# A decoder trunk on one core: three engines issue in the order of the text, and weights are split three units ahead

## The chip, the core and the metric

The kernel runs on one core of a Trainium2 chip. The metric is device time in microseconds (us) of one execution. The engines of the core are TensorE (PE: matrix products, into PSUM), VectorE (DVE), ScalarE (ACT), GpSimd (POOL) and SyncE (SP); each takes its instructions from a queue of its own, and DMA transfers are issued from the queues of SP, ACT and POOL. Here the weights' loads are issued from SP's queue.

## The reference

The input is 256 tokens of 2048 numbers in float32. There are two residual layers, each a mixer followed by a feed-forward part, and a last norm:

```
layer 0:  h = rms_norm(x);  z = h @ w_in
          y_a = rwkv7(z[:, :3360])      # 16 heads x 64: token shift, data-dependent decay,
                                        # S = S*w + (S a) b + v k per token, read with r, norm, gate
          y_b = diff_attention(z[...])  # 8 heads, two softmax maps each, rotary positions, 128-wide values
          x = x + concat(y_a, y_b) @ w_out
          h = rms_norm(x);  x = x + (silu(h @ w_gate) * (h @ w_up)) @ w_down    # hidden 5632
layer 1:  z = gelu(rms_norm(x) @ od_in);  u, v = split(z);  v = layer_norm(v)
          x = x + (u * (tril(w_s) v + b)) @ od_out      # w_s: 16 groups of 128 x 128, per chunk of 128 tokens
          h = rms_norm(x);  x = x + (silu(h @ w_gate) * (h @ w_up)) @ w_down
return rms_norm(x)
```

All weights are read once, 401 MB of them. They are float32, and the products are made to about that precision from pairs of a rounded half and a remainder.

## The kernel before, in words

**Tiles and units.** Activations lie transposed, features on the 128 partitions and the 256 tokens along the free axis. An activation tile `act` is 128x512: columns 0 to 255 hold the value rounded to the format fp32r (the hi half), columns 256 to 511 the remainder (the lo half). A projection (`proj_a`, L288) makes 256 output features and goes over its inputs in units of 256 input rows. For a unit, `weights` (L241) gives two parts hi and lo of the weights: ScalarE rounds the loaded tile `st` (L255, `hi`), and VectorE subtracts (L256, `lo`). A unit then has four products of `hi` with all 512 columns of `act` (L302) and four of `lo` with the first 256 (L306), into the PSUM tile `acc`. Every second unit, counted back from the last, does the lo products first, so that eight hi products follow one another. With `wide=False` the products are three times four of 256 columns (L314 to L316). `proj_b` (L327) turns the operands around for results with tokens on the partitions; its units are half as many rows and twice as many columns (L335 to L337).

**Buffers.** There are three `st` buffers of two units each (a load of 512 KB), five `hi`, five `lo`, two `acc` and four small PSUM tiles `sm`. `AHEAD` (L27) says how many split units `weights` keeps in hand beyond the one that it returns: with 1, the split of the next unit stands in the text before the products of this one.

**Stages.** Layer 0 begins with a projection that follows the loading of `x`, the sums of its norm, and the three evacuations that mix each token with the one before (`shifted`). Four quarters of the recurrent part (`quarter`) and two groups of attention (`rope`, `attention`) then run as generators beside the projections that deliver the next ones: after each unit `tick` (L272) advances the first lane by 1.3 steps and the second by 1.1, and `pause` yields steps in which nothing is done. In a quarter, GpSimd stores 8 small pieces of a product to DRAM, loads them back spread out as `DB` and writes ones on its diagonal (L629); VectorE's recursion over 15 rows (L696, L697) begins with that tile, thirteen paused steps and nine others later in the text. The feed-forward part (`ffn`, L424) has 22 pairs of a gate and an up projection of eight units; after the up projection of a pair come `comb_a` for the gate (ScalarE copies half of `acc`, L323; VectorE adds, L324, and multiplies by the norm, L325), Silu (L431), `comb_a` for the up projection, a product (L434) and the two casts and subtractions of the hidden tile (`split`, L285 and L286). Then `out_proj` (L412) has eight projections of 22 units, each followed by two adds to the residual (L414, L416) and, through `Norm.chunk`, by the casts and the square that prepare the next norm. `Norm.end` (L377) makes the reciprocal root from the sums. Layer 1 begins with the loads of two rows, biases and `w_s` on ScalarE's queue (L958, L963, L970); `mixers`, a generator, transposes `w_s` on TensorE (L973).

**What sets the order.** The functions record instructions in the order of the text. A scheduler then orders each engine's queue: it keeps dependencies and buffers, takes the order of the text as priority, and moves an instruction ahead of others that it expects not to be ready, by its own estimate of durations. The semaphores are set afterwards. On the chip every engine goes through its queue in that order.

Of the kernel before, what the change touches and what calls it, by code (L numbers as in the profile page):

```python
# [23 lines left out]
CDEC = math.exp(-0.5)  # L24
RATE_Q = 1.3
RATE_A = 1.1
AHEAD = 1  # L27
XLOAD = (2,2,2,2,2,2,2,2)
XFIRST = 2
Y1 = 2  # L30
# [100 lines left out]
def trunk_kernel(  # L131
# [15 lines left out]
    nc = tc.nc  # L147
    V, S, T, G = nc.vector, nc.scalar, nc.tensor, nc.gpsimd

    cpool = ctx.enter_context(tc.tile_pool(name="cpool", bufs=1))  # L150
    wpool = ctx.enter_context(tc.tile_pool(name="wpool", bufs=4))
    pool = ctx.enter_context(tc.tile_pool(name="pool", bufs=1))
# [88 lines left out]
    def weights(w, row, col):  # L241
        while len(ready) <= AHEAD and (halves or plan):
            if not halves:
                src, r, nr, c, ncol = plan.popleft()
                n = nr * ncol // 128
                st = wpool.tile([128, 1024], F32, tag="st", name=nm("st"), bufs=3)[:, :n]
                nc.sync.dma_start(st, wts[at[0] : at[0] + 128 * n].rearrange("(p f) -> p f", p=128))
                at[0] += 128 * n
                nh = 2 if nr == 512 or ncol > 256 else 1
                for h in range(nh):  # L250
                    halves.append((st[:, h * n // nh : (h + 1) * n // nh], n // nh, ncol, (src, r + h * nr // nh, c)))
            half, n, ncol, key = halves.popleft()
            hi = wpool.tile([128, 512], F32R, tag="hi", name=nm("hi"), bufs=5)
            lo = wpool.tile([128, 512], F32R, tag="lo", name=nm("lo"), bufs=5)
            S.copy(hi[:, :n], half)  # L255
            V.tensor_sub(lo[:, :n], half, hi[:, :n])  # L256
            ready.append(([(hi[:, k : k + ncol], lo[:, k : k + ncol]) for k in range(0, n, ncol)], key))
        parts, key = ready.popleft()
        assert key == (w, row, col), (key, w, row, col)
        return parts  # L260
# [872 lines left out]
```

## Time and profile before

| | |
|---|---|
| median of 3 runs | 2350.4 us (2349.5 to 2353.93) |
| profiled execution | 2349.51 us, span 2347.7 us, granted TensorE clock 0.992 of full |
| TensorE busy | 2291.3 us, 98% |
| VectorE, ScalarE, GpSimd busy | 1531.8, 1197.4, 66.4 us |
| DMA | 414.08 MB, 176 GB/s |

TensorE is the engine to look at: busy time of the others costs nothing while it works. Where it pauses, the timeline and the list of waits say what ended the pause. A line of the waits names the instruction that waited, the one that it waited for, the total, how often and the longest. TensorE's products are pipelined, so the distance between two starts says more than the length of one.

### The profile page before, as it was taken

The page shows a single profiled execution, that of the slowest core. Times are in us where ns is not written, and L with a number is a line of the kernel's source. Part 1 is how long each engine was busy: PE and PEld are TensorE (multiplying, and loading weights), DVE is VectorE, ACT ScalarE, POOL GpSimd, SP SyncE. Part 2 cuts the span into 40 slices and gives each one's busy share as a digit, 9 for nine tenths or more (in the row PEclk, how much of TensorE's full clock was granted, in tenths as well). Part 3 has the DMA queues.
Part 4 walks back from the last instruction along what each step waited for, and adds up shares of the span by engine and source line. Part 5 has one row for each costly group of instructions (what it writes and reads, how often), then busy time and mean ns, then how long its engine had stood idle before and what let it go on. Part 6 is the DMA issues. An engine that isn't in the chain of part 4 may idle for free.

```text
span 2347.7 us, 39701 instructions
## 1 busy us (share of the span) xinstructions
PE 2291.3 (98%) x14878; PEld 2008.8 (86%) x14878; DVE 1531.8 (65%) x2845; ACT 1197.4 (51%) x2230; POOL 66.4 (3%) x96
## 2 busy tenths in 40 slices
PE   8898989899999999999999999999999999999997
PEld 8887887688888888888888888888888888888887
DVE  7667776688766666665555558776666666665554
ACT  6445544556555555554444455555555555544443
POOL 0000000002000000000000000010000000000000
PEclk9999999999999999999999999999999999999999
DMA  6544344435566665656666765566666666656664
GB/s 217 144 135 123 117 124 146 115 113 185 183 189 189 188 189 188 189 189 188 189 189 188 244 194 176 177 188 181 192 190 189 187 188 191 190 189 189 189 189 135
DMA packets 121105, 414.08 MB, mean 176 GB/s; under 512 B 14160, under 2 KB 18384, under 8 KB 120400
## 3 DMA queue, kind: packets, MB, share of 16 engines
q1 hardware_dynamic: 113664, 401.00, 55.1%
q0 software_dynamic: 2112, 4.46, 0.9%
q10 hardware_dynamic: 5136, 6.09, 0.8%
q8 instruction: 116, 1.90, 0.3%
q14 instruction: 77, 0.63, 0.1%
HBM read 409.14 MB, written 2.36 MB: 175 GB/s over the span
## 4 chain that ended last, share of the span: by engine, by line
PE 77%; DVE 2%; issue 1%; DMA 1%; ACT 0%; POOL 0%; DVEq 0%; POOLq 0%; ACTq 0%
PE acc L302 46%; PE acc L306 24%; PE acc L314 1%; PE acc L315 1%; PE acc L316 1%; PE acc L337 1%; PE acc L336 1%; PE acc L335 1%; DVE lo L256 1%; ACT hi L255 0%; DMA AT<-in_w_s 0%; PE sm L1026 0%; DMA st<-in_wts 0%; PE sm L742 0%; DVE xres L1043 0%
## 5 line engine op out<-in xcount | busy, mean ns | idle before, releaser
L256 DVE TENSOR_TENSOR lo<-st,hi 128x512 fp32r<-128x512 f32 (+1 forms) x1520 | 1048.6, 694 | 618.6 <-ACT hi L255 613.8
L255 ACT CAST hi<-st 128x512 fp32r<-128x512 f32 (+1 forms) x1520 | 927.3, 618 | 947.3 <-PE acc L302 606.6
L302 PE MATMUL acc<-H,hi 128*128 128x512 f32 x3560 | 901.2, 393 | 0.0
L302 PEld LDWEIGHTS acc<-H,hi 128*128 128x128 f32 x3560 | 639.2, 189 | 113.3 <-issue 0.3
L306 PEld LDWEIGHTS acc<-H,lo 128*128 128x128 f32 x3560 | 486.2, 190 | 44.4 <-DVE lo L256 9.3
L306 PE MATMUL acc<-H,lo 128*128 128x256 f32 x3560 | 501.5, 283 | 9.1 <-DVE lo L256 9.1
L316 PE MATMUL acc<-H,lo 128*128 128x256 f32 x488 | 141.7, 290 | 14.6 <-DVE lo L256 14.5
L314 PE MATMUL acc<-H,hi 128*128 128x256 f32 x488 | 144.1, 295 | 8.4 <-ACT hi L255 8.4
L315 PE MATMUL acc<-H,hi 128*128 128x256 f32 x488 | 140.9, 289 | 0.0
L336 PE MATMUL acc<-lo,H 128*128 128x512 f32 (+1 forms) x320 | 126.1, 394 | 6.5 <-DVE lo L256 6.5
L335 PE MATMUL acc<-hi,H 128*128 128x512 f32 (+1 forms) x320 | 129.6, 405 | 0.0
L337 PE MATMUL acc<-hi,H 128*128 128x512 f32 (+1 forms) x320 | 125.7, 393 | 0.0
L316 PEld LDWEIGHTS acc<-H,lo 128*128 128x128 f32 x488 | 96.1, 197 | 15.9 <-DVE lo L256 15.5
L302 PE MATMUL acc<-AT,hi 128*128 128x512 f32 x400 | 105.7, 396 | 0.0
L314 PEld LDWEIGHTS acc<-H,hi 128*128 128x128 f32 x488 | 96.0, 197 | 11.2 <-ACT hi L255 8.4
L302 PE MATMUL acc<-RB,hi 128*128 128x512 f32 x392 | 101.7, 392 | 0.0
L324 DVE TENSOR_TENSOR TR<-acc,TA 128x512 f32<-128x512 f32 x96 | 66.0, 688 | 54.3 <-ACT TA L323 54.3
L315 PEld LDWEIGHTS acc<-H,hi 128*128 128x128 f32 x488 | 96.0, 197 | 0.6 <-issue 0.3
L323 ACT COPY TA<-acc 128x512 f32<-128x512 f32 x96 | 56.1, 584 | 60.6 <-PE acc L302 60.6
L302 PEld LDWEIGHTS acc<-AT,hi 128*128 128x128 f32 x400 | 72.0, 189 | 13.7 <-issue 0.3
L302 PEld LDWEIGHTS acc<-RB,hi 128*128 128x128 f32 x392 | 70.5, 189 | 12.8
L336 PEld LDWEIGHTS acc<-lo,H 128*128 128x128 f32 x320 | 61.1, 191 | 17.4 <-DVE lo L256 6.9
(330 smaller groups left out, 2057.4 us busy)
## 6 DMA issues: line engine op xcount, KB each, us to landing
st<-in_wts SPq DMA_DIRECT2D x740, 512.0 KB, 3.6
st<-in_wts SPq DMA_DIRECT2D x20, 256.0 KB, 2.7
DB<-scr POOLq DMA_DIRECT2D x4, 1024.0 KB, 13.7
st<-in_wts SPq DMA_DIRECT2D x8, 416.0 KB, 3.3
xres<-in_x SPq DMA_DIRECT2D x8, 256.0 KB, 5.8
RB<-in_rows ACTq DMA_DIRECT2D x8, 256.0 KB, 6.1
AT<-in_b_s ACTq DMA_DIRECT2D x4, 256.0 KB, 6.4
AT<-in_w_s ACTq DMA_DIRECT2D x4, 256.0 KB, 8.2
```

Of the source, the lines that this page charges most:

```text
L255: S.copy(hi[:, :n], half)
L256: V.tensor_sub(lo[:, :n], half, hi[:, :n])
L302: T.matmul(acc[:, m, :], hi, acts[2 * u + k], start=first and k == 0, stop=last and k == 1)
L306: T.matmul(acc[:, m, 0:256], lo, acts[2 * u + k][:, 0:256], start=False, stop=False)
L314: T.matmul(acc[:, m, 0:256], hi, act[:, 0:256], start=first and k == 0, stop=False)
L315: T.matmul(acc[:, m, 0:256], hi, act[:, 256:512], start=False, stop=False)
L316: T.matmul(acc[:, m, 0:256], lo, act[:, 0:256], start=False, stop=last and k == 1)
L323: S.copy(t3, acc[:, :nmt, 256:512])
L324: V.tensor_add(dst, acc[:, :nmt, 0:256], t3)
L335: T.matmul(acc[:, t, :ncol], xh, hi, start=k == 0, stop=False)
L336: T.matmul(acc[:, t, :ncol], xh, lo, start=False, stop=False)
L337: T.matmul(acc[:, t, :ncol], xl, hi, start=False, stop=k == last)
```

## The change

```diff
-AHEAD = 1
+AHEAD = 3
 XLOAD = (2,2,2,2,2,2,2,2)
...
     V, S, T, G = nc.vector, nc.scalar, nc.tensor, nc.gpsimd
 
+    ctx.enter_context(tc.manual_schedule(engines={mybir.EngineType.PE, mybir.EngineType.DVE, mybir.EngineType.Activation}))
     cpool = ctx.enter_context(tc.tile_pool(name="cpool", bufs=1))
```

TensorE, VectorE and ScalarE now issue their instructions as the text records them; the scheduler still orders the queues of SyncE and GpSimd. DMAs that ScalarE issues stand where the text has them too. `weights` splits three units ahead of the one it returns; the five hi and lo buffers are unchanged. The added line moves all later lines down by one, so that L255 becomes L256.

The first place is ScalarE's queue at the end of a pair of the first feed-forward layer. `TA<-acc` is the copy of half a projection's result, `TR<-TR` Silu, `H` a hidden tile, `hi` a rounded unit of weights. Before:

```order
L255 CAST hi_11763<-st_11761 128x512
L255 CAST hi_11794<-st_11761 128x512
L255 CAST hi_11808<-st_11806 128x512
L255 CAST hi_11820<-st_11806 128x512
L323 COPY TA_11782<-acc_11670 128x512
L255 CAST hi_11834<-st_11832 128x512
L255 CAST hi_11846<-st_11832 128x512
L255 CAST hi_11860<-st_11858 128x512
L255 CAST hi_11872<-st_11858 128x512
L285 CAST H_11787<-TR_11781 128x256
L285 CAST H_11790<-TR_11781 128x256
L255 CAST hi_11886<-st_11884 128x512
```

Now, for the same pair:

```order
L256 CAST hi_11749<-st_11747 128x512
L256 CAST hi_11761<-st_11747 128x512
L256 CAST hi_11775<-st_11773 128x512
L324 COPY TA_11788<-acc_11577 128x512
L432 ACTIVATE TR_11787<-TR_11787 128x512
L324 COPY TA_11794<-acc_11682 128x512
L286 CAST H_11799<-TR_11793 128x256
L286 CAST H_11802<-TR_11793 128x256
L256 CAST hi_11806<-st_11773 128x512
L256 CAST hi_11820<-st_11818 128x512
```

The copies, Silu and the casts of a pair stood between splits and stand now in one block, behind the splits of three units of the next pair and ahead of the fourth (`hi_11806`). The gate's copy and its Silu, which stood among the up projection's splits, have moved behind all of these.

The second place is VectorE's queue at the end of another pair of that layer. `TR<-acc,TA` is the add, `TR<-TR,rb` the product with the norm, `AT` and `H` are hidden tiles. Before:

```order
L324 TENSOR_TENSOR TR_11325<-acc_11214,TA_11326 128x512
L256 TENSOR_TENSOR lo_11379<-st_11376,hi_11378 128x512
L325 TENSOR_TENSOR TR_11325<-TR_11325,rb_7099 128x512
L256 TENSOR_TENSOR lo_11391<-st_11376,hi_11390 128x512
L434 TENSOR_TENSOR TR_11325<-TR_11325,TR_11319 128x512
L256 TENSOR_TENSOR lo_11405<-st_11402,hi_11404 128x512
L256 TENSOR_TENSOR lo_11417<-st_11402,hi_11416 128x512
L286 TENSOR_TENSOR AT_11331<-TR_11325,AT_11331 128x256
L286 TENSOR_TENSOR H_11334<-TR_11325,H_11334 128x256
L256 TENSOR_TENSOR lo_11431<-st_11428,hi_11430 128x512
```

Now:

```order
L257 TENSOR_TENSOR lo_11320<-st_11317,hi_11319 128x512
L325 TENSOR_TENSOR TR_11331<-acc_11121,TA_11332 128x512
L326 TENSOR_TENSOR TR_11331<-TR_11331,rb_7111 128x512
L325 TENSOR_TENSOR TR_11337<-acc_11226,TA_11338 128x512
L326 TENSOR_TENSOR TR_11337<-TR_11337,rb_7111 128x512
L435 TENSOR_TENSOR TR_11337<-TR_11337,TR_11331 128x512
L287 TENSOR_TENSOR AT_11343<-TR_11337,AT_11343 128x256
L287 TENSOR_TENSOR H_11346<-TR_11337,H_11346 128x256
L257 TENSOR_TENSOR lo_11351<-st_11317,hi_11350 128x512
```

The adds and products of both projections and the two subtractions have drawn together between the third unit's split and the fourth's.

The third place is ScalarE's queue where layer 1 begins. `AT<-in_b_s` are bias loads, `AT<-in_w_s` the four loads of `w_s`. Before:

```order
L963 DMA AT_14520<-in_b_s 128x512
L255 CAST hi_14473<-st_14471 128x512
L970 DMA AT_14535<-in_w_s 128x4x128
L255 CAST hi_14525<-st_14471 128x512
L970 DMA AT_14556<-in_w_s 128x4x128
L255 CAST hi_14546<-st_14544 128x512
L970 DMA AT_14575<-in_w_s 128x4x128
L255 CAST hi_14565<-st_14544 128x512
L970 DMA AT_14596<-in_w_s 128x4x128
L255 CAST hi_14586<-st_14584 128x512
L365 ACTIVATE H_14490<-xres,vc 128x256
```

Now:

```order
L350 ACTIVATE TA_14508<-xres 128x512
L959 DMA RB_14510<-in_rows 128x512
L959 DMA RB_14512<-in_rows 128x512
L959 DMA RB_14514<-in_rows 128x512
L959 DMA RB_14516<-in_rows 128x512
L959 DMA RB_14518<-in_rows 128x512
L959 DMA RB_14520<-in_rows 128x512
L959 DMA RB_14522<-in_rows 128x512
L959 DMA RB_14524<-in_rows 128x512
L964 DMA AT_14526<-in_b_s 128x512
```

Before, the twelve row and bias loads and the four of `w_s` stood between splits, ahead of the last casts and square of the old norm (L365). Now they follow that square (L350), all twelve in a row; behind three more bias loads come the split of a unit and the first load of `w_s`, and each later load of `w_s` behind one more split.

## Rows read from the trace of the kernel before

**Rows 1.** The page: busy us (share of the span) and instructions, by engine.
```profile
PE 2291.3 (98%) x14878; PEld 2008.8 (86%) x14878; DVE 1531.8 (65%) x2845; ACT 1197.4 (51%) x2230; POOL 66.4 (3%) x96
```

**Rows 2.** Busy time by stretch: engines, granted clock, DMA share, GB/s.
```profile
60.00:120.00 60.00, 52.09 (x430) 48.55 (x429) 38.45 (x98) 28.75 (x60) 5.26 (x10) 0.94 0.53 149
...
600.00:1000.00 400.00, 400.00 (x2292) 351.97 (x2292) 258.99 (x412) 210.01 (x376) 0.00 (x0) 1.00 0.62 190
```

**Rows 3.** Waits of TensorE: us in total, times, longest.
```profile
PE acc L316 <- DVE lo L256: 14.5, 3, 7.8
...
PE acc L306 <- DVE lo L256: 9.1, 1, 9.1
...
PE acc L336 <- DVE lo L256: 6.5, 1, 6.5
```

**Rows 4.** Timeline: start us, us, what [idle before], at the first quarter's L696.
```profile
107.17 0.17 DVE L696 TENSOR_TENSOR sub<-DB,inv 128x16 f32<-128x16 f32 x1 [11.73 <-POOL DB L629]
...
111.11 0.58 PE L316 MATMUL acc<-H,lo 128*128 128x256 f32 x1 [7.75 <-DVE lo L256]
...
111.49 0.41 PE L314 MATMUL acc<-H,hi 128*128 128x256 f32 x1
...
111.70 0.41 PE L315 MATMUL acc<-H,hi 128*128 128x256 f32 x1
...
115.26 0.28 PE L314 MATMUL acc<-H,hi 128*128 128x256 f32 x1
...
115.38 0.28 PE L315 MATMUL acc<-H,hi 128*128 128x256 f32 x1
```

**Rows 5.** Timeline: a boundary of the first feed-forward layer.
```profile
775.11 2.00 PE L302 MATMUL acc<-H,hi 128*128 128x512 f32 x8
...
776.24 0.59 ACT L323 COPY TA<-acc 128x512 f32<-128x512 f32 x1 [1.26 <-PE acc L302]
...
777.90 2.00 PE L302 MATMUL acc<-H,hi 128*128 128x512 f32 x8
```

**Rows 6.** Groups by form: busy us, mean ns of one, idle before.
```profile
L256 DVE TENSOR_TENSOR lo<-st,hi 128x512 fp32r<-128x512 f32 x1496 | 1035.8, 697 | 613.2 <-ACT hi L255 608.5 <-PE acc L315 1.5
...
L324 DVE TENSOR_TENSOR TR<-acc,TA 128x512 f32<-128x512 f32 x96 | 66.0, 688 | 54.3 <-ACT TA L323 54.3
...
L434 DVE TENSOR_TENSOR TR<-TR,TR 128x512 f32<-128x512 f32 x44 | 30.2, 685 | 0.0
...
L255 ACT CAST hi<-st 128x512 fp32r<-128x512 f32 x1496 | 915.8, 620 | 936.5 <-PE acc L302 606.6 <-PE acc L315 66.5 <-issue 62.8
...
L323 ACT COPY TA<-acc 128x512 f32<-128x512 f32 x96 | 56.1, 584 | 60.6 <-PE acc L302 60.6
...
L431 ACT ACTIVATE TR<-TR 128x512 f32<-128x512 f32 x44 | 27.6, 627 | 0.0
...
L285 ACT CAST RB<-TR 128x256 fp32r<-128x256 f32 x28 | 10.1, 401 | 0.0
```

**Rows 7.** Groups by form: a product of the norm's root.
```profile
L189 DVE TENSOR_TENSOR TR<-rb 128x256 f32<-128x256 f32 x12 | 5.1, 422 | 0.2
```

**Rows 8.** Timeline: ScalarE issues a row load.
```profile
1294.37 0.34 ACTq L958 DMA_DIRECT2D RB<-in_rows  x1
```

**Rows 9.** DMA issues: count, KB each, median us to landing.
```profile
DB<-scr POOLq DMA_DIRECT2D x4, 1024.0 KB, 13.7
...
RB<-in_rows ACTq DMA_DIRECT2D x8, 256.0 KB, 6.1
...
AT<-in_w_s ACTq DMA_DIRECT2D x4, 256.0 KB, 8.2
...
sk<-in_lam ACTq DMA_DIRECT2D x1, 128.0 KB, 4.5
```

**Rows 10.** Timeline of TensorE at the first transposes of w_s.
```profile
1316.00 0.66 PE L973 MATMUL sm<-c,AT 128*128 128x128 f32 x4 [1.57 <-DMA AT<-in_w_s]
...
1316.72 0.39 PE L336 MATMUL acc<-lo,H 128*128 128x512 f32 x1
```

## The prediction

> **What bounds the kernel now.** I read the page's busy shares first. TensorE is busy 2291.3 of the span's 2347.7 us [rows 1], so the whole idle time that any order of issue could give back is 56 us. The busy time by stretch says where it lies: in the feed-forward stretch from 600 to 1000 us TensorE is busy all 400, while between 60 and 120 us it is idle for 8 and its granted clock is 0.94 of the 2.4 GHz level [rows 2]. The waits of TensorE name what ends that idle time: a lo half from VectorE, 14.5, 9.1 and 6.5 us, with single waits of up to 9.1 [rows 3]. The timeline of one of them gives the cause. VectorE stood 11.73 us at L696, the recursion for the inverse, until GpSimd had written the ones into the gathered diagonal; every split queued behind it came late, TensorE waited 7.75 us, and the products that followed started 0.21 us apart (111.49, 111.70) where later ones start 0.12 apart (115.26, 115.38): 3.8 us at half rate, so the wait cost another 1.8 us [rows 4]. There is one such place in each of the four quarters. The rest of the kernel is a TensorE that never waits, because the evacuations of one projection stand between the splits of the next on ScalarE and VectorE.
>
> The sum is made against the profiled execution's own 2349.5 us, within 1 us of the median 2350.4.
>
> **What the change gives.** In the text, 22 steps of a quarter lie between the gather's loads and L696 (nine yields and the pause of 13). At 1.3 steps for each unit that is 17 units of 1.4 us, 24 us, and the quarter's own products lie between them too. The gather takes 13.7 us to land [rows 9] and the eight small loads before it several more, about 21 together, so VectorE should find it done. That takes away the three lines of [rows 3], 30 us, and four times 1.8 us of slow clock: **-37 us**. It can't be more than the idle total allows, and if a quarter's wait stays it is 9 less.
>
> **What it costs: the feed-forward boundary.** In the rows of the order, the gate's copy, its Silu, the up projection's copy and the two casts of the hidden tile now stand in one block on ScalarE, and the next split after them is that of the fourth unit of the next projection (U3). On VectorE the same holds of the add, two products, two subtractions. Let T0 be the end of the up projection. A unit is (777.90-775.11)/2 = 1.395 us and ScalarE sees TensorE's end 0.20 us late (two units are eight products of 512 columns and eight of 256, so four of 512 take a third of 2.79, 0.93; they start at 775.11 and end at 776.04, and the copy starts at 776.24) [rows 5]. The durations are those of [rows 6].
> The hi cast of U2 needs the buffer of the up projection's sixth unit, free at T0-2.79; it runs from -2.59 to -1.97. The gate's copy ends at -1.39, lo of U2 at -1.27, the add at -0.58, the product with the norm at 0.11, Silu at 0.74. Only then does ScalarE take the up projection's copy, to 1.32. The add ends at 2.01, the two products at 3.38, the two casts at 4.18, hi of U3 at 4.80, lo of U3 at 5.50. TensorE has U0 to U2, 3 x 1.395 = 4.18 us, and U3 is one of the units that begin with lo. It waits 1.3 us, with about 0.03 at each change of engine 1.5. There are 44 boundaries: 44 x 1.5 = **+66 us**. Low end: if the gate's part is out of the way when T0 comes, 0.5 less each, 41; high end 2.0 each, 88. After the wait ScalarE and VectorE need 1.3 of every 1.395 us at most and are three units ahead again before the next boundary.
>
> **Other projections.** At a boundary of an output projection the same chain is two adds, two scaled casts, a square and the split: 0.20 + 2 x 0.69 + 2 x 0.40 + 0.63 + 0.62 + 0.70 = 4.3 us (adds taken as long as L324, casts as L285, the square as L431 [rows 6]) against 4.18, hence 0.1 to 0.4 at about 30 boundaries. In the second pass over w_out a projection has only three units, 4.18 us, and VectorE 3 x 0.7 + 2 x 0.69 + 2 x 0.42 = 4.3 us of work: perhaps 0.8 each, eight times. Together +14 (6 to 24). The eight boundaries of the gated unit have copy, add, product, Gelu, add, product, casts and split, 6.3 us, less 4.18 and the mixing products: +10 (5 to 15).
>
> **Norms.** A norm's reciprocal root is thirteen VectorE operations of at most 0.42 us [rows 7], a chain of about 5 us that stood between splits before and is now one block. In the feed-forward layers U3 comes 1.9 us late, twice. Before the gated unit TensorE itself waits for the chain, 5.5 us, and loses 1.8 to the clock. Together +13 (8 to 18).
>
> **The start.** TensorE begins when four units are split rather than two, 3 us. The eight squares and fifteen adds of the first norm (8 x 2 x 0.42 = 6.7 us of VectorE) stand before the fourth unit of a projection with half-wide units, whose three units cover 2.1: 5 us. Then the norm's chain, on which TensorE waits 5.7; behind it ScalarE issues the load of the lambdas, 4.5 us to land [rows 9], VectorE waits for it, and three shifted evacuations (each some 2 us, two engines in turn) stand before U3: about 21 us from the end of the projection, of which three units cover 4.2. With two slow-clock stretches: 20. Together **+28** (12 to 40).
>
> **The loads of the gated unit.** ScalarE issues eight row loads and four bias loads, 0.34 us each [rows 8], then splits U3, then issues the first load of w_s, which takes 8.2 us [rows 9]; TensorE's transposes of it stand behind the projection's first unit. T0 + 3 for the last adds and casts, 4 for issuing, 0.6, 8.2 gives 16 us, and 20 if the later row loads must wait for the first to land (6.1). TensorE waits 14 to 18 us there, and the fourth of these loads is issued only when TensorE has gone on, some 5 us more. Before, it waited 1.57 [rows 10]. **+25** (12 to 30).
>
> **The recurrent and attention part.** Here the trace of before shows no such wait, since small products stood wherever their operands were ready. I walked one quarter. The four tanh, a split and two squares on ScalarE (about 0.5 each) stand before a product one unit later: 2 us. The small reciprocal root and a copy: 1. Five 512-wide VectorE operations, as long as the 0.685 of L434 [rows 6], four 256-wide ones and three splits stand between the transposes and the products that need them, 9 us against four units at most: 4 to 5. The inverse's thirty small operations, some 8 us with splits between them, in five steps: 2. Since the rate is 1.3, about 15 of 64 steps follow another directly, half of these hand a result from TensorE to another engine and back, 0.6 each: 4. That is 14 a quarter, 57, and eight attention heads and four rotary pairs delay VectorE by 2 to 4 us each, of which perhaps 1 shows: **+70**. Bounds: 20 if the pauses in the text cover most of it, 110 if attention delays every chain. I take 70, the value of the quarter walked.
>
> **Sum.** -37 + 66 + 14 + 10 + 13 + 28 + 25 + 70 = 189; 2349.5 + 189 = **2540 us**.
>
> **The clock as a rule.** After a wait of 1.57 us the products of 512 columns still took 0.39 and the clock stayed granted in full [rows 10], after 7.75 it did not [rows 4]; so I price the short feed-forward waits without a loss of clock. The Trainium skill (TensorE: Matmul & The Clock Gate, Part 1) says that the array's default state is throttled and that activity releases it, which speaks against any change that adds idle time; by it, repeated waits might lower the clock each time. This case's trace bears it out for the long wait alone.
>
> **Rivals.**
> - *The short waits lower the clock.* Each feed-forward boundary would lose another 1.8 us, 44 x 1.8 = 79: 2620 us. Against it stands [rows 10]. Chance 0.08.
> - *The pauses fit the text.* The recurrent part costs 20 rather than 70 and the start and loads half of theirs: 2540 - 50 - 27 = 2463, say 2460. For it: the steps and pauses are counted in units, which only an issue by the text keeps. Chance 0.14.
> - *Three units ahead hide the chain* (the other side). If the fourth unit's lo half were there before T0 + 4.18, the feed-forward part, two thirds of the kernel, would cost nothing, and with the 37 us given back and small costs at the start the time would be 2330. The point is 4.18 us; my chain is at 5.5 and would have to lose a quarter. Chance 0.06.
> - *The costs are right in kind but small, and cancel.* 2350. Chance 0.03.
> - That the change does not do what it says is excluded by the rows of the order.
>
> The forecast has 0.69, with 2460 to 2610 for itself. The bounds added up go from 2420 to 2645; all low or all high at once is unlikely, so the range is 2440 to 2620. A measurement can tell about 0.2%, 5 us: faster 0.06, same 0.03, slower 0.91.
>
> **What would show it.** In the profile after: in the feed-forward stretch TensorE busy for about 94% with a wait on the lo half of 1.3 to 1.7 us every 24; TensorE waiting for the w_s load for 15 us or more; a gap near the first norm; no wait of VectorE at L696 (one line further down there); a granted clock of 1.00 in the feed-forward stretch. I am wrong if the feed-forward stretch stays at full, or if most of the loss lies before 540 us.

## The result and the profile after

The changed kernel takes 2555.44 us (median of 4 runs, 2555.2 to 2556.05) against 2349.95 (4 runs of the kernel before on the same chip): a ratio of 1.0876, 95% interval 1.0855 to 1.0896. The forecast was 2540 with a range of 2440 to 2620. The lines of the kernel after stand one further down than those of before.

The page of the kernel after answers to [rows 1]:

```profile
PE 2352.3 (92%) x14878; PEld 2038.1 (80%) x14878; DVE 1562.5 (61%) x2845; ACT 1165.6 (46%) x2230; POOL 65.0 (3%) x96
```

The span is 2553.8, so TensorE is idle for 201.5 us where it was idle for 56.4: 145 of the 206 us are waits. The other 61 are busy time: the same 14878 products took longer, and the busy time and the clock by stretch say where. I cut both traces at the first product of each norm (the start, the first mixer, the first feed-forward layer with the loads of the gated unit, the gated unit, the second layer) and show first the kernel before, then the kernel after. The columns are the stretch and its length, the busy time of TensorE, its weight loads, VectorE, ScalarE and GpSimd, the granted clock, the DMA share and GB/s.

```profile
0.00:42.13 42.13, 32.81 (x243) 32.12 (x244) 27.62 (x68) 27.43 (x57) 0.20 (x4) 1.00 0.73 248
42.13:584.80 542.67, 510.74 (x4521) 435.25 (x4520) 390.88 (x991) 270.72 (x600) 33.44 (x53) 0.97 0.44 134
584.80:1338.31 753.51, 751.94 (x4367) 663.60 (x4366) 471.51 (x738) 383.63 (x671) 11.57 (x13) 1.00 0.62 193
1338.31:1603.75 265.44, 265.01 (x1484) 231.42 (x1483) 189.78 (x329) 142.73 (x250) 11.58 (x13) 1.00 0.60 183
1603.75:2347.70 743.95, 730.85 (x4271) 646.38 (x4269) 451.99 (x720) 372.92 (x652) 9.62 (x13) 0.99 0.60 184
```

```profile
0.00:51.73 51.73, 34.51 (x243) 33.10 (x244) 27.59 (x56) 27.72 (x55) 0.20 (x4) 0.93 0.56 189
51.73:675.90 624.17, 542.62 (x4521) 453.69 (x4520) 413.96 (x1002) 261.52 (x602) 32.11 (x53) 0.93 0.39 117
675.90:1481.58 805.68, 761.16 (x4367) 666.32 (x4366) 473.86 (x739) 374.80 (x671) 11.55 (x13) 0.99 0.57 181
1481.58:1772.61 291.03, 275.21 (x1483) 237.06 (x1482) 191.79 (x328) 136.91 (x251) 11.56 (x13) 0.98 0.51 166
1772.61:2553.80 781.19, 738.75 (x4271) 647.90 (x4269) 455.26 (x721) 364.68 (x652) 9.62 (x13) 0.99 0.55 176
```

Read the second column down both tables: the stretches grew by 9.6, 81.5, 52.2, 25.6 and 37.2 us. In the second, idle time went from 542.67 - 510.74 = 31.9 to 81.5 us, and busy time from 510.7 to 542.6 at a clock of 0.93. So half of the 61 us of busy time lies in the first mixer. In the two feed-forward stretches (the third and the fifth) the clock is at 0.99 and most of the loss is idle time, 43 and 29 us more, against 9 and 8 of busy time. In the gated unit, the fourth, it is 15 of idle and 10 of busy time, at a clock of 0.98 where it was 1.00.

The waits of TensorE after, answering to [rows 3]:

```profile
PE acc L307 <- DVE lo L257: 72.0, 80, 3.2
PE sm L974 <- DMA AT<-in_w_s: 15.4, 1, 15.4
PE acc L315 <- ACT hi L256: 15.2, 5, 5.5
PE sm L388 <- DVE rb L192: 11.1, 2, 5.6
PE sm L637 <- DVE TR L635: 8.7, 4, 4.4
PE sm L620 <- DVE BK L594: 7.1, 4, 2.7
```

The long waits of [rows 3] are gone: on their three lines (now L317, L307 and L337) no wait is over 3.2 us. In their place L307 has 80 short ones, and small products wait (L637, L620) that did not. The boundary of the feed-forward layer that the prediction worked out, after:

```profile
881.08 2.00 PE L303 MATMUL acc<-H,hi 128*128 128x512 f32 x8
882.12 0.63 ACT L432 ACTIVATE TR<-TR 128x512 f32<-128x512 f32 x1 [1.60 <-DVE TR L326]
882.66 0.57 ACT L324 COPY TA<-acc 128x512 f32<-128x512 f32 x1
...
883.26 0.69 DVE L325 TENSOR_TENSOR TR<-acc,TA 128x512 f32<-128x512 f32 x1 [1.17 <-ACT TA L324]
...
884.71 0.69 DVE L435 TENSOR_TENSOR TR<-TR,TR 128x512 f32<-128x512 f32 x1
885.44 0.71 ACT L286 CAST RB<-TR 128x256 fp32r<-128x256 f32 x2 [2.21 <-DVE TR L435]
...
885.71 0.63 PE L307 MATMUL acc<-H,lo 128*128 128x256 f32 x4
...
886.05 2.71 ACT L256 CAST hi<-st 128x512 fp32r<-128x512 f32 x5
886.70 1.89 DVE L257 TENSOR_TENSOR lo<-st,hi 128x512 fp32r<-128x512 f32 x3
...
887.45 0.74 PE L307 MATMUL acc<-H,lo 128*128 128x256 f32 x4 [1.11 <-DVE lo L257]
...
888.03 0.40 PE L303 MATMUL acc<-H,hi 128*128 128x512 f32 x1
```

TensorE ends the up projection at about 882.0. Its next three units were split beforehand; the fourth one's hi half starts at 886.05, behind Silu, copy and casts, its lo half at 886.70, and TensorE waits 1.11 us. Two Silu are now 23.71 us apart (858.41, 882.12). In the kernel before they stand 22.35 apart:

```profile
746.04 0.63 ACT L431 ACTIVATE TR<-TR 128x512 f32<-128x512 f32 x1
...
768.39 0.63 ACT L431 ACTIVATE TR<-TR 128x512 f32<-128x512 f32 x1
```

That is 1.36 per boundary, 0.25 more than the wait. The four products at 885.71 start 0.12 apart, so the next was due at 886.19 and starts 1.26 later; the wait is counted only from the end of the last product, 0.15 after that. The four behind the wait take 0.58 to the next line (888.03) where such four take 0.48: 0.10 more.

In a longer stretch of that layer TensorE is busy for 323.42 of 340 us, at a granted clock of 1.00:

```profile
720.00:1060.00 340.00, 323.42 (x1834) 282.11 (x1833) 209.98 (x332) 166.16 (x304) 0.00 (x0) 1.00 0.56 178
```

### The profile page after: what moved, and what is told of

It reads as the page before. It is cut to its first block, busy times and chain, and to the rows that moved or that the text cites. A ratio compares the mean times of both kernels' runs of the same rounds, so it can differ in the third digit from the quotient of the medians.

```text
span 2553.8 us, 39488 instructions
## 1 busy us (share of the span) xinstructions
PE 2352.3 (92%) x14878; PEld 2038.1 (80%) x14878; DVE 1562.5 (61%) x2845; ACT 1165.6 (46%) x2230; POOL 65.0 (3%) x96
## 4 chain that ended last, share of the span: by engine, by line
PE 55%; DVE 13%; ACT 6%; issue 2%; DMA 2%; ACTq 0%; DVEq 0%
PE acc L303 31%; PE acc L307 17%; DVE lo L257 5%; ACT hi L256 3%; DVE TR L326 2%; DVE TR L325 2%; DMA st<-in_wts 1%; PE acc L336 1%; PE acc L337 1%; PE acc L338 1%; DVE TR L435 1%; PE acc L317 1%; PE acc L315 1%; PE acc L316 1%; ACT TR L432 1%
## 5 line engine op out<-in xcount | busy, mean ns | idle before, releaser
L257 DVE TENSOR_TENSOR lo<-st,hi 128x512 fp32r<-128x512 f32 (+1 forms) x1520 | 1012.7, 695 | 725.4 <-ACT hi L256 715.8
L256 ACT CAST hi<-st 128x512 fp32r<-128x512 f32 (+1 forms) x1520 | 883.3, 616 | 772.1 <-PE acc L303 346.1
L303 PEld LDWEIGHTS acc<-H,hi 128*128 128x128 f32 x3560 | 639.7, 189 | 125.6 <-ACT hi L256 9.9
L307 PEld LDWEIGHTS acc<-H,lo 128*128 128x128 f32 x3560 | 489.5, 190 | 116.3 <-DVE lo L257 81.0
L307 PE MATMUL acc<-H,lo 128*128 128x256 f32 x3560 | 517.0, 284 | 66.8 <-DVE lo L257 66.8
L315 PE MATMUL acc<-H,hi 128*128 128x256 f32 x488 | 150.5, 308 | 25.3 <-ACT hi L256 15.2
L317 PE MATMUL acc<-H,lo 128*128 128x256 f32 x488 | 146.4, 300 | 6.4 <-DVE lo L257 6.2
L316 PE MATMUL acc<-H,hi 128*128 128x256 f32 x488 | 145.5, 298 | 0.2 <-DVE H L367 0.2
L336 PE MATMUL acc<-hi,H 128*128 128x512 f32 (+1 forms) x320 | 137.2, 429 | 0.0
L337 PE MATMUL acc<-lo,H 128*128 128x512 f32 (+1 forms) x320 | 129.2, 404 | 1.3 <-DVE lo L257 1.3
L338 PE MATMUL acc<-hi,H 128*128 128x512 f32 (+1 forms) x320 | 128.7, 402 | 0.0
L315 PEld LDWEIGHTS acc<-H,hi 128*128 128x128 f32 x488 | 100.9, 207 | 30.1 <-ACT hi L256 16.7
L317 PEld LDWEIGHTS acc<-H,lo 128*128 128x128 f32 x488 | 100.6, 206 | 9.2 <-DVE lo L257 9.1
L316 PEld LDWEIGHTS acc<-H,hi 128*128 128x128 f32 x488 | 100.8, 207 | 1.1 <-DVE H L367 0.9
L336 PEld LDWEIGHTS acc<-hi,H 128*128 128x128 f32 x320 | 63.5, 199 | 14.7 <-issue 2.1
L337 PEld LDWEIGHTS acc<-lo,H 128*128 128x128 f32 x320 | 63.9, 200 | 14.2 <-DVE lo L257 2.4
```

The source lines that it names most:

```text
L303: T.matmul(acc[:, m, :], hi, acts[2 * u + k], start=first and k == 0, stop=last and k == 1)
L307: T.matmul(acc[:, m, 0:256], lo, acts[2 * u + k][:, 0:256], start=False, stop=False)
L315: T.matmul(acc[:, m, 0:256], hi, act[:, 0:256], start=first and k == 0, stop=False)
L316: T.matmul(acc[:, m, 0:256], hi, act[:, 256:512], start=False, stop=False)
L317: T.matmul(acc[:, m, 0:256], lo, act[:, 0:256], start=False, stop=last and k == 1)
L336: T.matmul(acc[:, t, :ncol], xh, hi, start=k == 0, stop=False)
```

## The experiments

Each ratio is taken against the kernel before on the chip of that run, where it took 2349.95 to 2352.18 us; a difference between runs of two chips is good to about 2 us. Line numbers are those of the run's own kernel.

**Undo one part: three units ahead, order by the scheduler.** Kernel before with

```diff
-AHEAD = 1
+AHEAD = 3
```

> The kernel before with AHEAD = 3 alone; the scheduler still orders all engines. Theory (the order of issue costs, the number of units ahead does not): the scheduler moves splits ahead as far as the five buffers allow whatever the text says, so 2350 us within 0.5%, and TensorE in the feed-forward stretch busy throughout. Rival (splits three units ahead take VectorE and ScalarE from the side work): 2370 to 2400.

Measured: 2353.0 us, ratio 1.0006 (0.9997 to 1.0016). The longer lead alone does nothing; whatever the change costs, the order costs.

**Undo the other part: the text's order, one unit ahead.** Kernel after with

```diff
-AHEAD = 3
+AHEAD = 1
```

> The changed kernel with AHEAD = 1. Theory (a block between the splits is late by its length less the units in hand): each feed-forward boundary has two units less, 2.8 us more, 44 x 2.8 = 123; some 30 boundaries of output projections and 8 of the gated unit 2.8 more each, 106; the 24 projections of the recurrent part perhaps 2 each, 48: 2555 + 277 = 2830 (2760 to 2900), and TensorE's wait for lo at a feed-forward boundary 3.9 us instead of 1.1. Rival (units in hand matter little, the cost is side work in the queues): under 2620.

Measured: 2950.7 us, ratio 1.255 (1.2521 to 1.258), more than was expected. The block of evacuations is the same, two units less of products cover it. Its waits, one boundary, and the stretch 700 to 1300 (the last projections of the first mixer, then the feed-forward layer):

```profile
PE acc L307 <- DVE lo L257: 269.2, 93, 4.7
```

```profile
909.38 1.23 PE L307 MATMUL acc<-H,lo 128*128 128x256 f32 x4 [3.46 <-DVE lo L257]
```

```profile
700.00:1300.00 600.00, 510.47 (x2679) 440.77 (x2678) 327.08 (x513) 251.72 (x454) 11.47 (x13) 0.93 0.45 147
```

A boundary now waits 3.46 us, and the clock over the stretch is 0.93; from 800 to 1300, where there are boundaries alone, it is 0.93 too. That is the part which the expectation missed: with waits of 1.11 us the feed-forward clock was 1.00, with 3.46 in the same places it is not. Over the whole run the granted clock is 0.924, against 0.975 with three units ahead.

**The text's order in the feed-forward layers alone.** Kernel after, the region narrowed:

```diff
-    ctx.enter_context(tc.manual_schedule(engines=...))
+    with tc.manual_schedule(engines=...):
+        norm = ffn(0, norm, lambda: Norm("mix1"))
...
+    with tc.manual_schedule(engines=...):
+        fn = ffn(1, norm, Norm)
```

> AHEAD = 3, issue in the order of the text in the two feed-forward parts alone (with their down projections); the scheduler orders the rest. Theory (the feed-forward boundaries cost 1.4 us each by themselves): 44 x 1.38 = 61, two norms 2 x 1.9 with what follows 3 each, sixteen boundaries of the down projection 0.3 each: 2350 + 72 = 2422 (2405 to 2440). Rival (the boundaries are late because the stages before leave late loads): under 2380.

Measured: 2428.24 us, ratio 1.0328 (1.0307 to 1.0349): 77 us. With the scheduler's order in the mixer two of the lines of [rows 3] are back, and in the first line here the wait of 8.6 answers to their 9.1; the other 58 waits of that line, 56 us, are new:

```profile
PE acc L306 <- DVE lo L256: 64.5, 59, 8.6
PE acc L316 <- DVE lo L256: 14.9, 3, 8.1
```

**The text's order in the first mixer alone.** The region closes ahead of the first feed-forward layer:

```diff
+    part = ExitStack()
+    part.enter_context(tc.manual_schedule(engines=...))
...
+    part.close()
     norm = ffn(0, norm, lambda: Norm("mix1"))
```

> AHEAD = 3, order of the text from the start to the end of the first mixer's output projection, the scheduler from there on. Theory (the costs of the stages add up): from the two traces the changed kernel reaches the first norm 9.6 us later and the next norm another 81.5: 2350 + 91 = 2441 us (2430 to 2452). Rival (part of that loss is caused by what the next stage does or is made good there): under 2425 or over 2460.

Measured: 2436.39 us, ratio 1.0364 (1.0343 to 1.0385): 85 us, where the trace of the whole change showed 9.6 + 81.5 = 91. The stages roughly add: 77 + 85 = 162 of 205. Neither region reaches the gated unit and its loads, where the trace of the whole change has 25.6 us and the wait of 15.4, about the 43 that are left.

**One engine at a time in the text's order.** Three kernels, each the kernel after with one engine in the list:

```diff
-engines={mybir.EngineType.PE, mybir.EngineType.DVE, mybir.EngineType.Activation}
+engines={mybir.EngineType.DVE}
```

(then `Activation` alone, then `PE` alone).

> AHEAD = 3, VectorE alone in the order of the text. Theory: in the feed-forward boundary ScalarE's splits and copies are free to move, so VectorE's block alone is late by 0.4 to 0.9 us with the restart (add from 0.8 us after the up projection, two products, two subtractions, lo of U3 at about 4.8 against 4.18): 20 to 40. L696 is reached in its place, -37. The norms' chains and the evacuations in the recurrent part 10 to 40. 2365 us (2335 to 2400). Rival (one engine in the order of the text is enough to make all boundaries as late as three are): over 2430.

> AHEAD = 3, ScalarE alone in the order of the text. Theory: the copy no longer waits for a late Silu, but hi of U3 still stands behind the two casts, which need VectorE's three operations: lo of U3 at about 5.0, late by 0.8 and 0.3 for the restart: 44 x 1.1 = 48. The waits behind L696 stay; the loads of w_s are issued as late as in the changed kernel, 10 to 20. 2425 us (2395 to 2450). Rival (ScalarE, busy half of the time, has slack): under 2370.

> AHEAD = 3, TensorE alone in the order of the text. Theory: no cost in the feed-forward part; in the recurrent part some products wait for a result of a step before, 5 to 30 us in all, and the waits behind L696 stay: 2365 us (2345 to 2390). Rival (the order of TensorE is what makes the recurrent part slow in the changed kernel): 2400 to 2440.

Measured: VectorE alone 2499.57 us, ratio 1.0636 (1.0553 to 1.0718); ScalarE alone 2505.15, 1.066 (1.0628 to 1.0691); TensorE alone 2395.16, 1.0192 (1.0161 to 1.0223). The first two expectations failed (VectorE alone came out as its rival said), and the third run fell 5 us outside its range. The boundary with VectorE alone in the text's order says why:

```profile
882.56 0.62 ACT L256 CAST hi<-st 128x512 fp32r<-128x512 f32 x1 [0.78 <-ACT hi L256]
...
883.52 0.76 DVE L287 TENSOR_TENSOR RB<-TR,RB 128x256 fp32r<-128x256 f32 x2 [0.60 <-ACT RB L286]
...
884.20 3.09 DVE L257 TENSOR_TENSOR lo<-st,hi 128x512 fp32r<-128x512 f32 x5
884.93 0.74 PE L307 MATMUL acc<-H,lo 128*128 128x256 f32 x4 [1.08 <-DVE lo L257]
```

ScalarE, free to choose, made the hi half at 882.56; VectorE held the lo half behind the products and casts until 884.20, and TensorE waited its 1.08 us as if all three were bound. The block needs one engine only, either of the two, since each split passes both. The stretch from 720 to 1060, with VectorE alone bound and then with ScalarE alone, is as idle as with all three:

```profile
720.00:1060.00 340.00, 324.91 (x1843) 283.63 (x1842) 209.09 (x331) 165.39 (x301) 0.00 (x0) 1.00 0.57 180
```

```profile
720.00:1060.00 340.00, 323.42 (x1831) 281.99 (x1830) 210.68 (x333) 165.78 (x303) 0.00 (x0) 1.00 0.55 175
```

With TensorE alone bound, it is busy throughout:

```profile
720.00:1060.00 340.00, 340.00 (x1949) 299.14 (x1947) 219.48 (x349) 178.20 (x320) 0.00 (x0) 1.00 0.61 189
```

TensorE's own order costs 44 us, none of them in this stretch; VectorE still stands at L697 for GpSimd there, 39.0 us in four times. The three costs, 148, 154 and 44 us, do not add up to 205: two of them hold the same boundaries, about 60 us. What the rest of the 148 and 154 is was not taken apart.

**Move the block out of the way.** Kernel after, with the gate's evacuation recorded at the up projection's fourth unit and the up projection's at the second unit of the next gate projection, by a hook that the projection already has:

```diff
-            ag = proj_a(f"w_gate{layer}", 256 * mp, 256, norm.act)
+            ag = proj_a(f"w_gate{layer}", 256 * mp, 256, norm.act, ahead=at_unit(1, late))
...
-            au = proj_a(f"w_up{layer}", 256 * mp, 256, norm.act)
+            au = proj_a(f"w_up{layer}", 256 * mp, 256, norm.act, ahead=at_unit(3, [lambda ag=ag, g=g: gate(ag, g)]))
+            late.append(lambda mp=mp, au=au, g=g: up(mp, au, g))
```

> The changed kernel (three engines in the order of the text, AHEAD = 3) with the evacuations of the feed-forward pairs written elsewhere: the gate's at the fourth unit of the up projection, the up projection's at the second unit of the next gate projection, behind the split of its fifth unit. Theory: that split is then due 5 us after the block begins and no split is late, so 44 x 1.38 = 61 us go: 2495 us (2485 to 2512), and TensorE has no wait for lo in those stretches. Rival (the waits come from weight loads that arrive in bursts): over 2535.

Measured: 2495.84 us, ratio 1.062 (1.0585 to 1.0655), about 60 us less than the change. The same work, in the text's order on all three engines, with the splits between:

```profile
720.00:1060.00 340.00, 340.00 (x1950) 299.28 (x1949) 220.54 (x349) 173.80 (x319) 0.00 (x0) 1.00 0.58 190
```

So the 44 boundaries cost about 60 us, and it is the place of the evacuations in the text that costs them.

**Load w_s earlier.** Kernel after; the four loads of `w_s` go behind the bias loads, and their transposes begin eight units later:

```diff
+    for q in range(4):
+        wts4.append(slot("AT"))
+        nc.scalar.dma_start(r3(wts4[q], 4), w_s[4 * q : 4 * q + 4].rearrange("g t s -> t g s"))
...
-    start("ws", mixers())
```

> The changed kernel with the four loads of w_s issued directly behind the bias loads and their transposes begun eight units later, beside the second projection of the gated unit. Theory (TensorE stood for a load that ScalarE issued only behind twelve others and a split): 15.4 us of waiting and 2 of slow clock go, 2537 us (2531 to 2545). Rival (the wait is the block of loads on ScalarE itself, so the fourth unit's split is as late as the transposes were): 2547 to 2557.

Measured: 2548.41 us, ratio 1.084 (1.0819 to 1.0862): about 7 us less, not the 18 expected. The rival was right. In place of the wait for `w_s` stands

```profile
PE acc L336 <- ACT hi L256: 8.8, 1, 8.8
```

The timeline of ScalarE in the kernel after shows what is between:

```profile
1442.65 3.52 ACTq L959 DMA_DIRECT2D RB<-in_rows  x6
1446.21 2.69 ACTq L964 DMA_DIRECT2D AT<-in_b_s  x4
1448.99 0.62 ACT L256 CAST hi<-st 128x512 fp32r<-128x512 f32 x1 [5.77 <-DMA RB<-in_rows]
```

Twelve loads from 1441.80 to 1448.90 (the first two stand just ahead) hold ScalarE for 7 us, and no unit is split. The sixteen in a block of this run hold it longer, from 1440.31 to 1451.66.

**Spread the loads.** Kernel after; each of the sixteen loads is a step of the stream of side work, one for about each unit of the gated unit's first projections, `w_s` first, its transposes last:

```diff
     def mixers():
+        for q in range(4):
+            nc.scalar.dma_start(r3(wts4[q], 4), w_s[4 * q : 4 * q + 4].rearrange("g t s -> t g s"))
+            yield
+        for n in range(4):
+            nc.scalar.dma_start(bst[n], b_s[0, 512 * n : 512 * n + 512].partition_broadcast(128))
+            yield
...
```

> The changed kernel, with the twelve loads of rows and biases and the four of w_s recorded one at a time between the units of the gated unit's first projections (w_s first) instead of in one block, and the transposes of w_s recorded behind all of them. Theory: the 15.4 us wait of TensorE for w_s comes from the block, ScalarE issuing twelve loads (7 us, 1441.80 to 1448.90) and only then the load of w_s; spread, each load costs ScalarE 0.4 us within a unit of 1.4, all have landed before they are read, and the time falls by the wait and 1 to 2 us of slow clock, to 2538 (2534 to 2543), with no wait over 3 us left before the gated unit's first projection. Rival: the load moves the wait as an earlier load of w_s did, to the split behind it or to the transposes, and the time stays at 2547 to 2556 with a wait of 7 us or more near the first 16 units.

Measured: 2537.59 us, ratio 1.079 (1.0772 to 1.0808), about 18 less than the change. TensorE has no wait for a load left between 1440 and 1600. The longest wait there is

```profile
PE sm L388 <- DVE rb L192: 7.2, 1, 7.2
```

One step of the expectation was off: a wait over 3 us did remain, that of the gated unit's norm, 7.2 where it had been 5.6. The run changes three things at once: the loads are spread, `w_s` comes first, and its transposes come last. It does not tell which of them took the wait away.

**The gain without the order.** If the change's one benefit is that VectorE no longer stands at the inverse while GpSimd's gather lands [rows 4], it should be had with the scheduler's order: the kernel before, with the first product of the recursion held behind the split recorded just ahead of it.

```diff
-            V.tensor_sub(lo[:, :n], half, hi[:, :n])
+            split_at[0] = V.tensor_sub(lo[:, :n], half, hi[:, :n]).ins
...
+            with tc.issue_after(split_at[0]) if r == 1 else nullcontext():
+                V.tensor_mul(t, d4[:, :, r, 0 : r + 1], inv[:, :, 0 : r + 1])
```

> The kernel before (AHEAD = 1, scheduled) with one edge of order for each quarter: the first product of the inverse's recursion is issued behind the split recorded just before it. Theory (VectorE reached that product too early and held the splits up): most of the four waits, 29 us, and of the 7 us of slow clock go: 2315 us (2305 to 2335). Rival (the splits were late because the gather or GpSimd's write disturbs VectorE): 2345 to 2355.

Measured: 2332.16 us, ratio 0.9914 (0.9897 to 0.9931), faster than both kernels. Its longest waits of TensorE:

```profile
PE acc L315 <- ACT hi L256: 9.8, 2, 8.5
PE sm L890 <- DVE TB L886: 6.9, 4, 3.8
PE acc L336 <- ACT hi L256: 3.4, 1, 3.4
```

The long waits of [rows 3] are gone here too. The first line is the start; the second had 1.8 us in the kernel before and the third is new, and with smaller ones they make the gain 19 rather than the 35 that I had hoped for.

**The same, four steps earlier.**

```diff
-        yield from pause(Y7)
+        yield from pause(Y7 - 4)
+        behind = split_at[0]
+        yield from pause(4)
...
+            with tc.issue_after(behind) if r == 1 else nullcontext():
```

> As inverse_behind, with the edge drawn to the split recorded four steps earlier, so that the recursion may begin some 4 us sooner; in the order of two of the quarters it moves forward by three to six instructions against inverse_behind. Theory (what was left there are products that waited because the recursion then came too late): 2325 us (2312 to 2335). Rival (sooner brings the wait for GpSimd back): 2335 to 2352.

Measured: 2332.84 us, ratio 0.993 (0.9914 to 0.9947). Between these two places for the edge there is no difference that a measurement tells. The time lies at the high end of the range, but the theory is not borne out: the two waits stand as before, 6.9 us at the product that was L890 and 3.5 at L336. What causes them stays open.

## Why the prediction was right, and which terms were not

The direction, the mechanism and the time (15 us under) held. How near the time came is in part luck. The sum has nearly all of its 189 us as waits, since it gives back four slow stretches and pays for three; the trace has 145 us of waits and 61 of longer busy time. Too much waiting and too little loss of clock nearly cancel. The granted clock of the profiled executions (0.992 over 2347.7 us before, 0.975 over 2553.8 after) makes at most 45 of the 61, an estimate, and the 44 boundaries another 11 at 0.25 each.

Of the signs that it named, the wait on the lo half came out smaller (1.11, not 1.3 to 1.7); TensorE is busy for 95% of the feed-forward stretch (94 forecast), and the wait for `w_s` and the clock there are as said. Two of its sums do not come out: the low end of the boundaries is 44 x 1.0 = 44, not 41, and the terms of the norms give 2 x 1.9 + 5.5 + 1.8 = 11, not 13. And TensorE did wait elsewhere in the kernel before: 17 us of listed waits lie outside the three lines of [rows 3], 8.4 of them at the start. By its steps:

- **What the change gives, -37.** The 30 us of waits are gone: in the trace after no wait on the lines of [rows 3] is over 3.2 us, and VectorE does not stand at L697 for GpSimd. That VectorE standing there caused them is shown by the edge in the kernel before, which removes the same waits. The 7 us of slow clock that were to come with them can't be seen in the stretch, where the clock fell.
- **The feed-forward boundary, +66.** Measured 1.36 for each of 44, 60 us, and about 60 by moving the block. The chain that was worked out holds: the fourth unit's lo half was forecast 5.50 us after the end of the up projection and is ready at 887.39, 5.38 after it, and TensorE goes on 1.26 late where 1.32 was forecast. The 0.2 added for changes of engine was not there; 0.10 came from the slower first products, which had not been priced.
- **The loads of w_s, +25.** One wait of 15.42 (14 to 18 was forecast) and its slow clock: about 18 by spreading the loads. The second wait, 5 us for the fourth load, did not come: that load was issued at 1461.43, and its transposes ran at 1464.81.
- **The start, +28.** The stretch grew by 9.6 where 8 was forecast; behind it lie a wait of 5.5 for the norm and one of 5.54 at 72.01, where about 11 was forecast for the lambdas and shifted evacuations (21 less 4.2 of cover and 5.7 for the norm). About 21 and the slow clock.
- **Norms and the gated unit, +13 and +10.** The gated unit's norm makes TensorE wait 5.60 (5.5 forecast), the first boundary of each feed-forward layer 1.94 (1.9 forecast); the lo halves of the gated unit and the output projection behind it wait 10.0 in 16 times (10 was forecast). The stretch grew by 25.6 us in all, since its busy time rose by 10.2, of which 1.8 had been priced.
- **Output projections, +14.** In the second pass over `w_out` four boundaries in a row wait 1.46 to 1.48 (639 to 657), the two ahead of them 0.45 and 0.89, where 0.8 was forecast. Those of the down projection wait 0.17 to 0.23 (0.1 to 0.4 forecast).
- **The recurrent and attention part, +70.** This is the mis-sized term. Of the 81.5 us of idle time in the stretch, 11 belong to the start (5.5 + 5.54) and about 9 to `w_out`; some 61 are left where 70 was forecast, 42 of them waits of the small products of quarters and heads and the others late splits of the projections beside them. So the waits were sized a little too large, and the clock was priced at nothing: busy time in the stretch rose by 31.9 us, though the four slow stretches of before had gone. At most 27 of these are the clock, an estimate from the two granted clocks (0.03 of 542.67 us lost before, 0.07 of 624.17 after). The timeline of TensorE after shows what one wait does there, the wait of 5.54 and the products behind it:

```profile
72.01 0.58 PE L315 MATMUL acc<-H,hi 128*128 128x256 f32 x1 [5.54 <-ACT hi L256]
...
73.33 0.41 PE L316 MATMUL acc<-H,hi 128*128 128x256 f32 x1
73.54 0.41 PE L317 MATMUL acc<-H,lo 128*128 128x256 f32 x1
...
75.34 0.28 PE L317 MATMUL acc<-H,lo 128*128 128x256 f32 x1
75.46 0.28 PE L315 MATMUL acc<-H,hi 128*128 128x256 f32 x1
```

Products start 0.21 us apart for 3 us, then 0.12. In the feed-forward part, with one wait of 1.11 every 24 us, the granted clock stayed 1.00, so the rival of short waits that lower the clock was wrong there. In the first mixer, with 64 waits of up to 5.5 us in 624, it was in part right (0.93), and there waits no longer than those of the feed-forward part are followed by the lower level. One of them, and the clock behind it:

```profile
97.22 1.23 PE L563 MATMUL sm<-c,TR 128*128 128x2 f32 x8 [1.16 <-ACT TR L559]
```

```profile
99.20:102.50 3.30, 3.30 (x12) 2.89 (x11) 1.85 (x11) 1.25 (x3) 0.00 (x0) 0.50 0.00 0
```

TensorE waited 1.16 us, ran eight products of two columns and a few of the projection, and then stood at 0.50 of full, the 1.2 GHz level. In the gated unit a wait of 2.07 us (1566.72) is followed by 0.50 as well, from 1566.9 to 1570.0. So the step that priced short waits without a loss of clock held in the feed-forward part and failed in these two. The Trainium skill (TensorE: Matmul & The Clock Gate, Part 1) takes the throttled state as the array's default, which activity releases; the wait of 5.54 at 72.01 agrees with that, and the waits of 1.11, at 1.00 throughout, do not show it.

The rival in which three units hide the chain failed at its own point: 4.18 us of cover against a chain of about 5.4. The rival in which the text's pauses fit failed in the first mixer, 85 us in all.

Not separated by a run: how much of the first mixer's 85 us belongs to each kind of small product, what divides the short waits that lowered the clock from those that did not, and whether the slow clock would go with a few of the waits or only with most.

## What to carry to other kernels

An engine that issues in the order of the text runs a block of evacuations as a block, and a lead of some units hides it only if their products last as long as the whole chain through both engines; work out that chain from the end of the projection to the half that is needed next, and spread the block between the splits (a lead longer than three was not run). DMA issues count in that chain too: twelve in a row held ScalarE for 7 us, and spreading the sixteen loads, `w_s` first and its transposes last, gave back 18. Where a scheduler's order is bad at one place, mend that place with one edge: it gave 0.9%, and the order of the whole text took 8.8%.

## What the runs showed that I had not expected

- One engine in the text's order is enough for the whole boundary wait (TensorE busy 324.91 of 340 us with VectorE alone, 323.42 with ScalarE alone, 323.42 with all three).
- A wait listed as 1.11 us costs 1.36, with the granted clock at 1.00 throughout: the next product starts 1.26 late, and the four behind the wait take 0.10 longer.
- The length of a wait alone does not tell what it does to the clock: 1.11 us every 24 us left it at 1.00, 3.46 us in the same places made it 0.93 over 600 us, and 1.16 us among the small products of the first mixer was followed by 3.3 us at 0.50.
